# Attention in turns of two head pairs: the order of scores, transposes and weighted sums

## The chip, the cores and the metric

The kernel runs on one core of a Trainium2 chip. The metric is the device time of one execution in microseconds (us), as a median of several runs. Matmuls and transposes run on TensorE (PE), element-wise work on VectorE (DVE), ScalarE (ACT) and GpSimd (POOL); transfers are issued from SyncE (SP) and ACT.

## What is computed

One layer of an encoder block on 1024 tokens of width 1024, a grid of 16 rows by 64 columns:

```python
h = rms_norm(x, norm1_g)
a, gate, q, k, v = split(h @ w_in)
conv_out = conformer_conv(a, gate, ...)             # 31 taps, layer norm, swish
q, k = rms_norm(q per head), rms_norm(k per head)   # 8 heads of 64
attn_out = neighbourhood_attention(q, k, v, rpb)
x = x + concat(conv_out, attn_out) @ w_out
x = x + swiglu(rms_norm(x, norm2_g))                # d_ff 2816
```

In the neighbourhood attention each query attends to 8 rows by 16 columns of keys, clamped inside the grid, with a learned bias by offset, a softmax and a weighted sum of the values:

```python
s = einsum("bqhd,brqchd->bhqrc", q_r, k_win) * scale + bias
p = softmax(s, axis=(-2, -1))
out = einsum("bhqrc,brqchd->bqhd", p, v_win)
```

## The kernel before

Every engine's instructions stay in the order in which the program issues them. A wait at the head of an engine's queue therefore holds all that is behind it on that engine.

The stages follow each other: the input projections with the convolution's taps beside them, the attention, the first output projection, the second norm, the SwiGLU products and the down projection. The stage of this change is the attention, some 80 us of the 1061.5 us of the profile.

There the 1024 queries are cut into 8 blocks of 128 (two halves of the grid's rows by four column blocks). Each block works on 12 grid rows of keys and on a column window of 24 columns for the outer column blocks (288 scores a query) or 32 for the inner ones (384). The blocks with 24 columns come first (`order`, line 600). A block has four head pairs, so there are 32 pairs, numbered `i`; 0 to 15 have 288 scores a row, 16 to 31 have 384.

For one pair:

- `score_mm(i)` (line 603): two matmuls with 64 contraction rows into two PSUM banks of the four that carry the tag `mm` (tile `s`).
- `score_exp(i, ss)` (616): for each head, DVE adds the bias table, writes to the SBUF tile `e` and gives the row's negative maximum (`mx`, line 624). ACT takes the exponential and its sum (626). `e` is a tile of the pool `G`, 128 x 1024 fp32, with 22 buffers.
- `score_norm(i)` (629): DVE's reciprocal of the two sums, POOL's scaling of both halves of `e` (633).
- `flip(i)` (635): six transposes of `e` to the PSUM tile `p`, two banks with the tag `cv`, of which there is a single one.
- `flip_out(i, hh)` (645): the copy of `p` to the SBUF tile `pT`, also of the pool `G`. Half 1 is ACT's, half 0 DVE's. The halves lie interleaved in `pT`:

```python
        (dve.tensor_copy, act.copy)[hh](pTs[i][:, :, hh], pp[i][:m, hh * 512:hh * 512 + 384].rearrange(
            "p (n q) -> p n q", q=P))
```

- `weigh(i)` (650): six matmuls with 64 output columns of `pT` by the values (`vw`), accumulated in the PSUM tile `o` of the block (tag `tp`, two banks).
- After the last pair of a block, `evac_hi` (661, ACT) and `evac_lo` (667, DVE, in two halves) take `o` to SBUF as a rounded part and its rest.

The loop at line 785 does one pair a turn: scores of pair i, transposes and copies of i-2, exponentials of i, weighted sums of i-3. Beside it, `jobs` (a weight split in quarters: a cast on ACT, a subtraction on POOL) go one at a time in two turns of four. After the last scores, `fill` puts the first steps of the output projection between the remaining groups, and then `conv_T` transposes the convolution's output (line 724), the first block of it to the same PSUM tile `cv` that the transposes of the attention use.

Of the kernel before, what the change touches and what calls it, by code (L numbers as in the profile page):

```python
# [12 lines left out]
P = 128  # L13
# [48 lines left out]
def body(tc, a):  # L62
    from contextlib import ExitStack
    with ExitStack() as ctx:
        build(ctx, tc, a)


def build(ctx, tc, a):
    nc = tc.nc
# [6 lines left out]
    def T(tag, shape, bufs, name, dt=F32):  # L76
        return sb.tile(shape, dt, tag=tag, bufs=bufs, name=name)

    def G(name, dt=F32):
        return T("G", [P, 1024], 22, name, dt)  # L80

    def R(name):
        return T("R", [P, 1024], 3, name)
# [7 lines left out]
    def SM(name, n=8):  # L91
        return T("sm", [P, 8], 16, name)[:, :n]

    def mm(name):
        return ps.tile([P, 512], F32, tag="mm", bufs=4, name=name)

    def tp(name):
        return ps.tile([P, 512], F32, tag="tp", bufs=2, name=name)

    def cv(name):  # L100
        return ps.tile([P, 1024], F32, tag="cv", bufs=1, name=name)
# [54 lines left out]
    def take_parts(jobs, n=4, sub=pool):  # L156
        i = pos[1]
        hi, lo = chunks[i][2]()
        w = 1024 // n

        def part(o):
            sl = slice(o, o + w)
            split(hi[:, sl], lo[:, sl], raws[i][:, sl], (sub,))
            if o + w == 1024:
                raws.pop(i)
                issue()
        pos[1] += 1
        jobs.extend(lambda o=o: part(o) for o in range(0, 1024, w))

    def g_pair(name, into):  # L170
        def dst():
            hl = (G(name + "h", F32R), G(name + "l", F32R))
            into.append(hl)
            return hl
        return dst
# [35 lines left out]
    def load_x(t):  # L211
        x_t[t] = G(f"x{t}")
        nc.sync.dma_start(x_t[t], a["x"][t * P:(t + 1) * P, :])

    def load_xt(h, kp, sl):
        if (h, kp) not in xr:
            xr[h, kp] = G(f"xt{h}{kp}").rearrange("p (k s) -> p k s", s=512)
        nc.sync.dma_start(xr[h, kp][:, :, sl], a["xt"][h, kp][:, :, sl])
# [328 lines left out]
    ss = SM("s14", 4)  # L547
# [27 lines left out]
    def table(rh, ty):  # L575
        n = AR * t1[ty].shape[-1]
        src = tf[rh, ty].rearrange("i j h c -> (i j) (h c)")
        if rh == 0 and ty == 0:
            parts = [(G(f"tab{k}")[:, :n * min(3, NH - 3 * k)], 3 * k) for k in range(3)]
        else:  # L580
            parts = [(H(f"tab{rh}{ty}")[:, :NH * n], 0)]
        heads = []
        for w, h0 in parts:
            nc.sync.dma_start(w, src[:, h0 * n:h0 * n + w.shape[-1]])
            heads += [w[:, o:o + n] for o in range(0, w.shape[-1], n)]
        return heads
# [14 lines left out]
    tab, es, pTs, os_, at, sums, pp = {}, {}, {}, {}, {}, {}, {}  # L601

    def score_mm(i):
        s_, hp = divmod(i, 4)
        rh, cb = order[s_]
        t = rh * 4 + cb
        c0, ncol, _ = WIN[cb]
        out = []
        for hh in range(2):
            s = mm(f"s{i}{hh}")[:, :AR * ncol]  # L610
            pe.matmul(s, qT[hh * HD:(hh + 1) * HD, hp, t * P:(t + 1) * P],  # L611
                      k4[hh * HD:(hh + 1) * HD, hp, rh * 4:rh * 4 + AR, c0:c0 + ncol], start=True, stop=True)
            out.append(s)
        return out

    def score_exp(i, ss):
        s_, hp = divmod(i, 4)
        rh, cb = order[s_]
        n = AR * WIN[cb][1]
        e = es[i] = G(f"e{i}").rearrange("p (h n) -> p h n", h=2)[:, :, :n]  # L620
        rs = SM(f"rs{i}", 2)
        for hh in range(2):
            mx = SM(f"mx{i}{hh}", 1)
            dve.tensor_tensor_reduce(out=e[:, hh], in0=ss[hh], in1=tab[rh, cb][2 * hp + hh], scale=-1.0,  # L624
                                     scalar=3.0e38, op0=OP.add, op1=OP.min, accum_out=mx)
            act.activation(e[:, hh], e[:, hh], AF.Exp, bias=mx, scale=-1.0, accum_out=rs[:, hh:hh + 1])  # L626
        sums[i] = rs

    def score_norm(i):
        rs = sums.pop(i)  # L630
        dve.reciprocal(rs, rs)  # L631
        for hh in range(2):
            pool.tensor_scalar(es[i][:, hh], es[i][:, hh], rs[:, hh:hh + 1], 1.0, op0=OP.mult, op1=OP.mult)  # L633

    def flip(i):
        s_, hp = divmod(i, 4)
        m = 4 * WIN[order[s_][1]][1]
        pp[i] = cv(f"p{i}")
        for hh in range(2):
            pt = pp[i][:, hh * 512:hh * 512 + 384]  # L640
            for g in range(3):
                pe.transpose(pt[:m, g * P:(g + 1) * P], es[i][:, hh, g * m:(g + 1) * m], ident)  # L642
        pTs[i] = G(f"pT{i}").rearrange("p (n h q) -> p n h q", h=2, q=P)[:m, :3]

    def flip_out(i, hh):
        m = pTs[i].shape[0]
        (dve.tensor_copy, act.copy)[hh](pTs[i][:, :, hh], pp[i][:m, hh * 512:hh * 512 + 384].rearrange(  # L647
            "p (n q) -> p n q", q=P))

    def weigh(i):  # L650
        s_, hp = divmod(i, 4)
        rh, cb = order[s_]
        if hp == 0:
            os_[s_] = tp(f"o{s_}").rearrange("p (c q) -> p c q", c=4)
        for g in range(3):
            for hh in range(2):
                c = (2 * hp + hh) * HD
                pe.matmul(os_[s_][hh * HD:(hh + 1) * HD, hp], vw[cb, rh + g][:, c:c + HD], pTs[i][:, g, hh],  # L658
                          start=g == 0, stop=g == 2)

    def evac_hi(s_):
        rh, cb = order[s_]
        if rh == 0:
            at[cb] = [G(f"at{cb}{w}", F32R).rearrange("p (c t q) -> p c t q", c=4, t=2) for w in range(2)]
        act.copy(at[cb][0][:, :, rh], os_[s_])

    def evac_lo(s_, cs=slice(0, 4)):
        rh, cb = order[s_]
        hi, lo = [w[:, cs, rh] for w in at[cb]]
        dve.tensor_tensor(lo, os_[s_][:, cs], hi.bitcast(F32), OP.subtract)  # L670
# [5 lines left out]
    jobs = []  # L676

    def load_window(cb):
        for g in range(4):
            load_vw(cb, g)  # L680
# [14 lines left out]
    for g in range(3):  # L695
        load_vw(0, g)
    score_exp(0, s0)
    s1 = score_mm(1)
    value(7)
    score_norm(0)  # L700
    score_exp(1, s1)
    step()
    load_vw(0, 3)
# [12 lines left out]
    def proj(t, d, acc, ks):  # L716
        for k in ks:
            mac(acc, lhs(k, t), wo[d, k], k == 4, k == 3)
            weave()
# [59 lines left out]
    def fill(*ks):  # L779
        if not acc0:  # L780
            act.activation(warm, eps, AF.Sqrt)
            acc0.append(mm("pj0"))
        proj(0, 0, acc0[0], ks)

    for i in range(2, 32 + 2):
        if i == 5:
            tab[0, 1] = tab[0, 2] = table(0, 1)
        if i == 9:
            tab[1, 1] = tab[1, 2] = table(1, 1)
        if i in (6, 12):  # L790
            load_window(i // 6)
        if i in (14, 22):
            take_parts(jobs)
        if i < 32:
            ss = score_mm(i)
        if i >= 32:
            fill(*((4, 5) if i == 32 else (6,)))
        if i < 33:
            score_norm(i - 1)
        flip(i - 2)  # L800
        flip_out(i - 2, 1)
        if i < 32:
            score_exp(i, ss)
        flip_out(i - 2, 0)
        if i > 2:
            weigh(i - 3)
            if i % 4 == 2:
                evac_hi(i // 4 - 1)
            elif i > 6 and i % 4 in (0, 3):
                evac_lo((i + 1) // 4 - 2, slice(0, 2) if i % 4 == 3 else slice(2, 4))  # L810
        if jobs and i % 4 < 2:
            jobs.pop(0)()
    fill(7)

# [401 lines left out]
    for s, p in enumerate(SEQ):  # L1216
        for k in range(QF - 2):
            n = s * QF + k
# [21 lines left out]

# [12 lines left out]
```

## Time and profile before

| | |
|---|---|
| median of 3 runs | 1063.39 us (1062.58 to 1063.52) |
| the profiled execution: time | 1063.23 us |
| its span from the first instruction to the last | 1061.5 us |
| PE busy | 1045.5 us |
| DVE busy | 703.9 us |
| ACT busy | 450.9 us |
| POOL busy | 383.8 us |
| attention, first transposes (pair 0) to the last (pair 31) | 239.65 to 314.01 us |

Times in the rows are us from the span's start unless they are marked ns. A row of the timeline has the start, the duration, the engine, the line, the operation, and output and inputs by the program's names; xN merges N instructions that follow each other. In brackets stands how long the engine was idle before, and what ended that. In the chain of waits each piece starts where the one before ceases to hold the end.

### The profile page before, as it was taken

To read this page: it belongs to the slowest core of one execution; us is meant where nothing else is said; L and a number is where in the kernel's file an instruction comes from. 1 tells how busy PE (TensorE), PEld (TensorE's weight loads), DVE (VectorE), ACT (ScalarE), POOL (GpSimd) and SP (SyncE) were. 2 spreads that over 40 slices of the span, in tenths; PEclk is the share of its full clock that TensorE was granted. 3 is DMA by queue.
4 is the path that set the end of the run, shared out by engine and by line. 5 is a ranking of instruction groups with operands and counts; after the bars stand their busy time and mean duration, and the time that the engine had idled before them with its cause. 6 is when DMAs were issued, how large, how long until landed. Compare 5 with 4: busy or idle time off the path is not lost.

```text
span 1061.5 us, 14053 instructions
## 1 busy us (share of the span) xinstructions
PE 1045.5 (98%) x5068; PEld 847.8 (80%) x5068; DVE 703.9 (66%) x1055; ACT 450.9 (42%) x987; POOL 383.8 (36%) x301
## 2 busy tenths in 40 slices
PE   7999999999999999999999999999999999999997
PEld 6888888876667887788888888888888888888886
DVE  6788987877765257666465564564655567858883
ACT  6456347726766234532323223232233344433441
POOL 0126765523542302444554544545444200002310
PEclk9999999999999999999999999999999999999999
DMA  9416781245504422032322323232231597634541
GB/s 333 165 49 224 223 256 38 77 151 159 165 30 161 137 100 80 23 127 83 134 96 96 109 99 102 97 129 100 70 134 75 198 320 275 208 99 137 188 141 42
DMA packets 68245, 144.06 MB, mean 136 GB/s; under 512 B 12496, under 2 KB 21200, under 8 KB 67536
## 3 DMA queue, kind: packets, MB, share of 16 engines
q1 hardware_dynamic: 66336, 139.95, 39.2%
q10 hardware_dynamic: 1840, 3.22, 0.9%
q8 instruction: 40, 0.66, 0.3%
q14 instruction: 29, 0.24, 0.1%
HBM read 103.99 MB, written 44.76 MB: 140 GB/s over the span
## 4 chain that ended last, share of the span: by engine, by line
PE 92%; DVE 5%; ACT 1%; issue 0%; DMA 0%; SPq 0%; DVEq 0%; ACTq 0%
PE B L113 5%; PE B L114 5%; PE B L112 5%; PE D L112 4%; PE D L114 4%; PE D L113 4%; PE A L112 4%; PE A L113 3%; PE A L114 3%; PE z L112 3%; PE z L113 3%; PE z L114 3%; PE gl L114 3%; PE gl L112 3%; PE gl L113 3%; DVE cv L319 3%
## 5 line engine op out<-in xcount | busy, mean ns | idle before, releaser
L319 DVE SCALAR_TENSOR_TENSOR cv<-u,par,cv 128x1009 f32<-128x1009 f32 (+14 forms) x92 | 117.5, 1277 | 2.4
L345 POOL TENSOR_TENSOR pa<-pa,pr 128x1022 f32<-128x1022 f32 (+5 forms) x24 | 58.0, 2415 | 50.8 <-ACT pr L344 35.2
L104 ACT CAST op<-sr 128x512 fp32r<-128x512 f32 x77 | 47.7, 619 | 50.2 <-PE B2d L114 21.3
L108 DVE TENSOR_TENSOR op<-sr,op 128x512 fp32r<-128x512 f32 x77 | 58.2, 756 | 14.8 <-ACT op L104 14.8
L1036 DVE TENSOR_TENSOR g<-B,g 128x512 f32<-128x512 f32 x22 | 15.2, 690 | 79.0 <-PE B L114 79.0
L1208 POOL TENSOR_TENSOR ou<-ou,resm 128x512 f32<-128x512 f32 x8 | 13.1, 1651 | 142.7 <-ACT op L104 135.0
L1045 ACT ACTIVATE D<-D 128x512 f32<-128x512 f32 x22 | 12.8, 582 | 112.8 <-DVE D L1044 112.8
L1031 DVE TENSOR_TENSOR u<-B,g 128x512 f32<-128x512 f32 x22 | 15.2, 691 | 62.0 <-PE B L114 62.0
L104 ACT CAST op<-wd 128x512 fp32r<-128x512 f32 x66 | 40.9, 619 | 33.5 <-DVE wd L1123 18.6
L108 DVE TENSOR_TENSOR op<-wd,op 128x512 fp32r<-128x512 f32 x66 | 49.7, 753 | 3.0 <-ACT op L104 1.3
L889 DVE TENSOR_TENSOR ts<-gu,ts 128x512 f32<-128x512 f32 x44 | 51.0, 1159 | 0.8
L633 POOL TENSOR_SCALAR e<-e,rs 128x288 f32<-128x288 f32 (+1 forms) x64 | 34.1, 545 | 45.9 <-DVE rs L631 37.1
L1034 ACT ACTIVATE A<-A 128x512 f32<-128x512 f32 x20 | 11.6, 582 | 76.3 <-PE A L114 76.3
L626 ACT ACTIVATE e<-e,mx 128x288 f32<-128x288 f32 (+1 forms) x64 | 36.2, 569 | 7.3 <-DVE mx L624 7.3
L889 DVE TENSOR_TENSOR ts<-gu 128x512 f32<-128x512 f32 x22 | 33.6, 1528 | 0.0
L624 DVE CUSTOM_DVE_ANT_0 e<-s,tab 128x288 f32<-128x288 f32 (+1 forms) x64 | 29.9, 504 | 3.6 <-PE s L611 3.6
L642 PEld LDWEIGHTS p<-ident,e 128*96 128x96 f32 (+1 forms) x192 | 20.1, 133 | 15.0 <-issue 10.4
L372 ACT ACTIVATE sq<-z,r 128x64 f32<-128x64 f32 x96 | 28.6, 334 | 6.5 <-PE z L114 6.5
L642 PE MATMUL p<-ident,e 128*96 128x128 f32 (+1 forms) x192 | 27.6, 280 | 0.6 <-DVE pT L647 0.6
L658 PE MATMUL o<-pT,vw 96*64 96x128 f32 (+1 forms) x384 | 28.0, 281 | 0.0
L611 PE MATMUL s<-kT,qT 64*128 64x288 f32 (+1 forms) x128 | 27.5, 495 | 0.5 <-DVE mx L624 0.5
L344 ACT ACTIVATE pr<-u,par 128x1022 f32<-128x1022 f32 (+5 forms) x24 | 27.0, 1137 | 1.6 <-ACT vs L402 1.6
(1038 smaller groups left out, 3452.6 us busy)
## 6 DMA issues: line engine op xcount, KB each, us to landing
gu<-in_gu SPq DMA_DIRECT2D x44, 512.0 KB
sr<-sd SPq DMA_DIRECT2D x77, 256.0 KB
sd<-sd SPq DMA_DIRECT2D x22, 512.0 KB
wd<-in_wd SPq DMA_DIRECT2D x44, 256.0 KB
sd<-g SPq DMA_DIRECT2D x33, 256.0 KB
x<-in_x SPq DMA_DIRECT2D x16, 512.0 KB
xd<-x SPq DMA_DIRECT2D x8, 512.0 KB
resm<-xd SPq DMA_DIRECT2D x16, 256.0 KB
```

Of the source, the lines that this page charges most:

```text
L104: act.copy(hi, src)
L108: eng.tensor_tensor(*[w[..., sl] for w in (lo, src, hi.bitcast(F32))], OP.subtract)
L112: pe.matmul(acc, lh, rh, start=start, stop=False, skip_group_check=True)
L113: pe.matmul(acc, lh, rl, start=False, stop=False, skip_group_check=True)
L114: pe.matmul(acc, ll, rh, start=False, stop=stop, skip_group_check=True)
L319: dve.scalar_tensor_tensor(acc[:, o], uc[:, i], dwk[:, c, t:t + 1], acc[:, o], OP.mult, OP.add)
L345: pool.tensor_tensor(pa[:, o], pa[:, o], pr[:, o], OP.add)
L624: dve.tensor_tensor_reduce(out=e[:, hh], in0=ss[hh], in1=tab[rh, cb][2 * hp + hh], scale=-1.0, scalar=3.0e38, op0=OP.add, op1=OP.min, accu ...
L626: act.activation(e[:, hh], e[:, hh], AF.Exp, bias=mx, scale=-1.0, accum_out=rs[:, hh:hh + 1])
L633: pool.tensor_scalar(es[i][:, hh], es[i][:, hh], rs[:, hh:hh + 1], 1.0, op0=OP.mult, op1=OP.mult)
L642: pe.transpose(pt[:m, g * P:(g + 1) * P], es[i][:, hh, g * m:(g + 1) * m], ident)
L889: dve.tensor_tensor(o, l, r, OP.subtract)
```

## The change

The loop takes two pairs a turn (i = 2, 4, ... 32): scores of i and i+1, transposes of i-2, weighted sums of i-3 and i-2, transposes of i-1. `score_exp` can be called for one head, and its calls are placed between the copies: first head 0 of pair i, then ACT's copy of pair i-2, then head 1 of pair i and head 0 of pair i+1, then DVE's copy of pair i-2; head 1 of pair i+1 and the normalization of pair i come after the weighted sums. The evacuations of `o` and the weight split come at the end of a turn. The bias tables are asked for at i = 4 and 8 (before: 5 and 9). The pool `G` has 24 buffers (before: 22), for which the reserve of SBUF for the DMA descriptors that software makes is set to 64 bytes a partition.

```diff
     def G(name, dt=F32):
-        return T("G", [P, 1024], 22, name, dt)
+        return T("G", [P, 1024], 24, name, dt)
...
-    def score_exp(i, ss):
+    def score_exp(i, ss, heads=(0, 1)):
...
-        e = es[i] = G(f"e{i}").rearrange("p (h n) -> p h n", h=2)[:, :, :n]
-        rs = SM(f"rs{i}", 2)
-        for hh in range(2):
+        if i not in es:
+            es[i] = G(f"e{i}").rearrange("p (h n) -> p h n", h=2)[:, :, :n]
+            sums[i] = SM(f"rs{i}", 2)
+        e, rs = es[i], sums[i]
+        for hh in heads:
...
-    for i in range(2, 32 + 2):
-        if i == 5:
+    for i in range(2, 32 + 2, 2):
+        last = i == 32
+        if i == 4:
             tab[0, 1] = tab[0, 2] = table(0, 1)
-        if i == 9:
+        if i == 8:
             tab[1, 1] = tab[1, 2] = table(1, 1)
...
-        if i < 32:
-            ss = score_mm(i)
-        if i >= 32:
-            fill(*((4, 5) if i == 32 else (6,)))
-        if i < 33:
-            score_norm(i - 1)
+        ss = [] if last else [score_mm(i), score_mm(i + 1)]
+        if last:
+            fill(4, 5)
+        score_norm(i - 1)
         flip(i - 2)
+        if not last:
+            score_exp(i, ss[0], (0,))
         flip_out(i - 2, 1)
-        if i < 32:
-            score_exp(i, ss)
+        if not last:
+            score_exp(i, ss[0], (1,))
+            score_exp(i + 1, ss[1], (0,))
         flip_out(i - 2, 0)
         if i > 2:
             weigh(i - 3)
-            if i % 4 == 2:
-                evac_hi(i // 4 - 1)
-            elif i > 6 and i % 4 in (0, 3):
-                evac_lo((i + 1) // 4 - 2, slice(0, 2) if i % 4 == 3 else slice(2, 4))
-        if jobs and i % 4 < 2:
+        if last:
+            fill(6)
+        weigh(i - 2)
+        if not last:
+            score_exp(i + 1, ss[1], (1,))
+            score_norm(i)
+        flip(i - 1)
+        flip_out(i - 1, 1)
+        flip_out(i - 1, 0)
+        if i % 4 == 2 and i > 2:
+            evac_hi(i // 4 - 1)
+        if i > 4:
+            evac_lo((i + 2) // 4 - 2, slice(0, 2) if i % 4 == 2 else slice(2, 4))
+        if jobs:
             jobs.pop(0)()
     fill(7)
...
-    nc = bacc.Bacc("TRN2", target_bir_lowering=False, num_devices=1)
+    nc = bacc.Bacc("TRN2", target_bir_lowering=False, num_devices=1, dynamic_dma_scratch_size=64)
```

More of the change, by code (lines that the diff above doesn't have):

```diff
@@ L626, in score_exp @@
             act.activation(e[:, hh], e[:, hh], AF.Exp, bias=mx, scale=-1.0, accum_out=rs[:, hh:hh + 1])
-        sums[i] = rs
     def score_norm(i):
```

## The prediction

> **What bounds the kernel now.** I read the page first: the engines' shares and the granted clock.
>
> ```profile
> span 1061.5 us, 14053 instructions
> ...
> PE 1045.5 (98%) x5068; PEld 847.8 (80%) x5068; DVE 703.9 (66%) x1055; ACT 450.9 (42%) x987; POOL 383.8 (36%) x301
> ...
> PEclk9999999999999999999999999999999999999999
> ```
>
> TensorE (PE) is busy for 98% of the span at full granted clock, so whatever is added between two of its instructions is added to the end. The second view is the table of windows; a stretch of the attention stage shows (busy us of PE, weight load, DVE, ACT, POOL, then clock):
>
> ```profile
> 290.00:300.00 10.00, 10.00 (x96) 6.47 (x92) 7.61 (x28) 7.95 (x25) 6.10 (x11) 1.00 0.15 50
> ```
>
> PE has no gap there, while DVE and ACT are at 76% and 80%. These two are close enough to full that their order inside a turn matters. The third view, the chain of waits in order of time, shows how long each group of PE work lasts. I call a pair's two score matmuls S (line 611), its six transposes F (642), its weighted sums W (658), ACT's and DVE's copies of the transposes A and D (647). D writes the half `hh` 0, A the half 1 of the same tile.
>
> ```profile
> 238.97 0.69 PE s L611 x4
> 239.65 0.81 PE p L642 x6
> 240.54 0.48 ACT pT L647
> 241.04 0.56 DVE pT L647
> 241.74 0.83 PE p L642 x6
> ...
> 257.08 0.69 PE s L611 x4
> 257.77 0.79 PE p L642 x6
> 258.56 0.81 PE o L658 x12
> ...
> 285.49 0.85 PE s L611 x4
> 286.34 0.81 PE p L642 x6
> 287.15 0.81 PE o L658 x12
> ...
> 308.46 0.81 PE p L642 x6
> ...
> 314.01 0.66 PE p L642 x6
> ...
> 316.38 0.44 PE y L724 x4
> ```
>
> Columns: start, duration, who. A pair costs 0.69 + 0.79 + 0.81 = 2.29 us with the narrow windows (288 scores a row, pairs 0 to 15) and 0.85 + 0.81 + 0.81 = 2.47 with the wide ones (384). All of it is PE's own work. The first five rows are the one place where PE must wait for the copies: F(0) starts at 239.65, A(0) follows 0.89 later, D(0) 0.50 after A(0), and F(1), which needs the same PSUM tile, 0.70 after D(0). From the start of F to the first PE instruction that needs both copies are 0.89 + 0.50 + 0.70 = 2.09 us. D does not run beside A, it runs behind it. The list of waits says so too (waiter, awaited: us, times, longest):
>
> ```profile
> DVE pT L647 <- ACT pT L647: 7.0, 16, 1.7
> ```
>
> After its start-up the old order hides the 2.09: behind F(i) come W(i-1), S(i+3), F(i+1), W(i), so W(i) starts 0.79 + 0.81 + 0.69 + 0.79 = 3.08 us after F(i), and F(i+1) 0.79 + 0.81 + 0.69 = 2.29 after it.
>
> **The change, part by part.** A turn (even i) becomes, on PE: S(i), S(i+1), F(i-2), W(i-3), W(i-2), F(i-1). I use line numbers of before.
>
> *Fewer group changes.* Transposes that follow their like or long matmuls without an edge take 0.66 for six (row 314.01), between S and W 0.79: an edge of some 0.13. If merging two W saves one edge and nothing else, PE's turn is 2 x 0.69 + 0.79 + 0.81 + 0.66 + 0.79 = 4.43 narrow, against 2 x 2.29 = 4.58, and 2 x 0.85 + 0.81 + 0.81 + 0.66 + 0.81 = 4.79 wide against 4.94. Over 14 turns (6 narrow, 8 wide) that is 14 x 0.15 = 2.1 us; the edges F to S and W to F that the new order has are not in the trace, nearest are these, and if two whole edges go each turn it is 14 x 0.26 = 3.6. The Trainium skill, TensorEngine Tiling (Array Packing), Key Properties, says that a change of tiling mode drains TensorE; scores (64 rows), transposes and sums (64 columns) are three modes, so by that rule alone the change is faster. The rows agree that there is an edge.
>
> *W(i-2) now follows F(i-2) with only W(i-3) between.* That is a cover of 0.79 + 0.81 = 1.60 against the 2.09 that the two copies need: PE idles at least 0.49 a turn, even if ACT and DVE are free when F ends. This already exceeds the edge saved. Behind the waiting W stand F(i-1) and everything else of PE.
>
> *ACT and DVE are not free then.* Both engines keep their program order. On ACT the new order is E(i,0), A(i-2), E(i,1), E(i+1,0), E(i+1,1), A(i-1), then evac_hi's cast and a weight cast; E is the exponential (626). On DVE: reciprocal(i-1), T(i,0), T(i,1), T(i+1,0), D(i-2), T(i+1,1), reciprocal(i), D(i-1), L; T is the bias and maximum (624), L the half evacuation of line 670. So A(i-2) stands behind E(i,0), that behind T(i,0), that behind reciprocal, L and D(i-1) of the turn before, and D(i-1) behind A(i-1) and F(i-1). F(i-1) in turn stands behind W of its turn. This closes a loop, F(i-1) to F(i+1), that runs once a turn. Its links, start to start:
>
> ```profile
> 254.59 0.55 DVE L647 COPY pT<-p 96x384 f32<-96x384 f32 x1 [0.30 <-ACT pT L647]
> 255.07 0.41 DVE L670 TENSOR_TENSOR at<-o,at 128x256 fp32r<-128x256 f32 x1
> 255.64 0.17 DVE L631 RECIPROCAL rs<-rs 128x2 f32<-128x2 f32 x1 [0.16 <-ACT e L626]
> 255.79 0.46 DVE L624 CUSTOM_DVE_ANT_0 e<-s,tab 128x288 f32<-128x288 f32 x1
> ```
>
> ```profile
> 232.04 0.45 DVE L624 CUSTOM_DVE_ANT_0 e<-s,tab 128x288 f32<-128x288 f32 x1
> ...
> 232.59 0.54 ACT L626 ACTIVATE e<-e,mx 128x288 f32<-128x288 f32 x1 [6.82 <-DVE mx L624]
> ```
>
> ```profile
> 259.56 0.52 ACT L626 ACTIVATE e<-e,mx 128x288 f32<-128x288 f32 x1
> 259.98 0.19 ACT L626 ACTIVATION_READ_ACCUMULATOR e<-e,mx 128x1 f32 x1
> 260.07 0.57 ACT L665 CAST at<-o 128x512 fp32r<-128x512 f32 x1
> ```
>
> ```profile
> L624 DVE CUSTOM_DVE_ANT_0 e<-s,tab x64: 439/505/558, 232.0 to 309.2; 128x288 f32<-128x288 f32 x32, 128x384 f32<-128x384 f32 x32
> L626 ACT ACTIVATE e<-e,mx x64: 520/568/619, 232.6 to 310.3; 128x288 f32<-128x288 f32 x32, 128x384 f32<-128x384 f32 x32
> ```
>
> F to A 0.89; A to D 0.50; D to L 0.48 (254.59 to 255.07); L to reciprocal 0.33 (its 0.41 less the 0.07 by which the next instruction overlapped D; an estimate); reciprocal to T 0.15; T to E 0.55 (232.04 to 232.59); E to the next on ACT 0.51 (259.56 to 260.07); A(i-2) to D(i-2) 0.50; D(i-2) to W(i-2) 0.70; W to F 0.83 (a group begun after a wait took 0.83 in row 241.74; W alone 0.66 to 0.84). Sum 5.44 us. With wide windows T and E are each longer, by the least and largest of the last two rows 0.10 and, as the next group starts before its end, some 0.09: 5.63. Both exceed PE's 4.43 and 4.79, so the loop sets the pace and PE idles 1.01 and 0.84 us a turn before W(i-2). S(i), S(i+1), F(i-2), W(i-3), 1.38 + 0.79 + 0.81, lie in its shadow.
>
> The sum from F(1) to F(29) (rows 241.74 and 308.46): 14 loops, 6 narrow, of which the first two have no L (0.33 less), 8 wide: 2 x 5.11 + 4 x 5.44 + 8 x 5.63 = 77.0 us. Before 66.7. Added: 10.3. Both spans hold 28 W.
>
> *The first turn* has no W(i-3): S(2) at 238.97, F(0) 1.38 later at 240.35, W(0) 2.09 later at 242.44, F(1) 0.83 later at 243.27, against 241.74: added 1.5.
>
> *The end.* After F(29) one W less is left (0.81 gained). The first four transposes of line 724 need the PSUM tile that D(31) empties. They started 2.37 after F(31) (314.01 to 316.38), with W(30) between, which now lies ahead of F(31): 1.56 by PE, 2.09 by the copies, so 0.5 is lost. Net 0.3 gained.
>
> *What costs nothing.* The scaling on POOL for F(i) now starts in the turn before, a whole S, S earlier than its use. Tables and value windows are asked for at most a pair earlier; no wait of PE in this stage ends on a DMA. The weight casts go from two pairs in four to one a turn, after A(i-1), where ACT has some 1.6 us until E(i+2,0). The four score banks are all taken each turn; S(i+2) follows T(i+1,1) by more than a group. The two more wide tiles hold one more e and one more pT, which the new order keeps alive. The reserve for software DMA descriptors shrinks, and the page's queues are hardware and instruction queues alone. Later stages are PE's own work, so the shift is carried to the end undiminished.
>
> Total: 10.3 + 1.5 - 0.3 = 11.5, from a span of 1061.5 to 1073.0. The profiled execution took 1063.23, 1.7 more than its span and 0.2 less than the median 1063.39. Forecast: 1074.9 us, 1.1% slower.
>
> **The rivals.** *Only the bare latency (chance 0.06).* If ACT came free in time, the turn would be 1.38 + 2.09 + 0.83 + 0.79 = 5.09 narrow and 1.70 + 2.10 + 0.83 + 0.81 = 5.44 wide: 74.1 against 66.7, with the ends 8.6 more, 1072.0. Against it: E(i,0) stands ahead of A(i-2) in program order.
>
> *No stall, edges saved (0.06): not slower.* If the copies were hidden, 2.1 to 3.6 us go: 1059.8 to 1061.3, faster by 0.2 to 0.3%. It decides where A and D together take under 1.60 us from F's start. Only running them side by side could do that, and the row 7.0, 16 speaks against it. This is also where the Trainium skill's drain rule would end if nothing else counted.
>
> *A buffer wait (0.03).* If the new e tile of pair i took the buffer that F(i-2) still reads, T(i,0) would wait for F(i-2): turn 1.38 + (0.89 + 0.55 + 0.51 + 0.50 + 0.70) + 0.83 + 0.79 = 6.15, wide 6.68, 25 us more, 1088. Against it: the number of tiles grows by just what the order needs.
>
> *The clock falls (0.02).* If PE's pauses of 1 us lowered its clock to half in the stage, its 4.43 and 4.79 would double and pass the loop: 6 x 8.86 + 8 x 9.58 = 129.8, some 63 more, 1126. Against it: no slice of the clock row is under 9. The Trainium skill, TensorE: Matmul & The Clock Gate, A second HAM failure mode, tells of short pauses between groups that throttled a kernel; no row here shows it.
>
> **How the numbers follow.** The loop has 0.83. Its own range: terms read from single rows, 0.3 a turn either way (L 0.33 or 0.41, W 0.66 or 0.84, a few hundredths for each wait), is 4 us: 1071 to 1079. The bare latency lies inside; a little more room above for waits not seen gives 1071 to 1080. Within 0.2% (2.1 us), about what can be told from no change, lies at most the near end of the second rival: same 0.01, faster 0.05, slower 0.94.
>
> **What would show it.** After the change the windows of the attention stage should show PE busy some 80 to 85% and DVE and ACT a lower share than before; the list of waits should name W (line 659 then) waiting for pT's copies on DVE some 15 times, about 1 us each, where none did; F(i-1) to F(i) should take about 2.2 us and F(i) to F(i+1) 3.3 (2.5 and 3.1 wide), together 5.4 then 5.6; A(i-2) should start right after E(i,0). The forecast is wrong if D starts before A's end, if the two F distances add to under 5.0, or if the time is gained back in another stage.

## The result and the profile after

The changed kernel takes 1073.64 us (median of 5, 1073.53 to 1073.91) against 1063.39 (1062.58 to 1064.02) of the kernel before on the same chip: 1.0098 times as long, 95% interval 1.0087 to 1.0108. The profiled execution took 1073.65 us with a span of 1071.7, against 1063.23 and 1061.5.

First the page of the kernel after: span, busy time with share and instructions of each engine, PE's busy share in 40 slices, and the granted clock.

```profile
span 1071.7 us, 14103 instructions
...
PE 1043.5 (97%) x5068; PEld 848.3 (79%) x5068; DVE 702.8 (66%) x1055; ACT 451.6 (42%) x987; POOL 383.7 (36%) x301
...
PE   7999999998889999999999999999999999999997
...
PEclk9999999999999999999999999999999999999999
```

PE has the same 5068 matmuls and is busy 2.0 us less than before, while the span is 10.2 us longer: the time went into pauses. They lie in slices 10 to 12, the only ones inside the span under 9; at 26.8 us a slice these cover 241 to 322 us, the attention stage. The clock row doesn't fall.

The same stretch of the attention stage in the table of windows (busy us of PE, weight load, DVE, ACT, POOL, then clock, DMA share, GB/s), and the list of waits (waiter, awaited: us in all, times, longest):

```profile
290.00:300.00 10.00, 9.11 (x84) 6.25 (x86) 6.29 (x25) 6.77 (x21) 5.42 (x9) 1.00 0.25 85
```

```profile
DVE pT L648 <- ACT pT L648: 35.7, 32, 2.5
...
PE o L659 <- DVE pT L648: 10.6, 15, 1.2
```

The window had 10.00 us of PE work (x96) before and has 9.11 (x84). DVE fell from 76% to 63%, ACT from 80% to 68%: they, too, do less in the same time. DVE now waits for ACT's copy for every one of the 32 pairs, 35.7 us where it was 7.0 for 16, and the weighted sums (659) wait for DVE's copy 15 times, 0.7 us each on average; before there was no such line.

One turn in the chain of waits, from F(i-1) to F(i+1):

```profile
258.70 0.79 PE p L643 x6
259.49 0.73 PE s L611 x4
...
261.45 0.63 ACT e L628 x2
262.08 0.37 ACT pT L648
...
262.47 0.56 DVE pT L648
...
263.08 0.88 PE o L659 x12
263.95 0.80 PE p L643 x6
```

And what DVE and ACT did in between, from the timeline of the same kernel:

```profile
260.03 0.55 DVE L648 COPY pT<-p 96x384 f32<-96x384 f32 x1 [1.81 <-ACT pT L648]
260.51 0.41 DVE L671 TENSOR_TENSOR at<-o,at 128x256 fp32r<-128x256 f32 x1
260.84 0.15 DVE L632 RECIPROCAL rs<-rs 128x2 f32<-128x2 f32 x1
260.91 0.43 DVE L626 CUSTOM_DVE_ANT_0 e<-s,tab 128x288 f32<-128x288 f32 x1
```

```profile
259.53 0.47 ACT L648 COPY pT<-p 96x384 f32<-96x384 f32 x1 [0.72 <-PE p L643]
261.45 0.54 ACT L628 ACTIVATE e<-e,mx 128x288 f32<-128x288 f32 x1 [1.45 <-DVE mx L626]
261.89 0.19 ACT L628 ACTIVATION_READ_ACCUMULATOR e<-e,mx 128x1 f32 x1
261.98 0.46 ACT L648 COPY pT<-p 96x384 f32<-96x384 f32 x1
```

Read them as one path: F(i-1) at 258.70, A(i-1) 259.53, D(i-1) 260.03, L 260.51, reciprocal 260.84, T(i,0) 260.91, E(i,0) 261.45, A(i-2) 261.98, D(i-2) 262.47, W(i-2) 263.08, F(i+1) 263.95. ACT is idle for 1.45 us ahead of E(i,0), though F(i-2) is about to hand it a copy; the copy stands behind that exponential in ACT's order. PE resumes 0.61 us after D(i-2) starts.

Where the 10.2 us of span went is read off the chain at the two ends of the stage:

```profile
239.23 1.53 PE s L611 x8
240.75 0.81 PE p L643 x6
...
243.63 0.80 PE p L643 x6
```

```profile
318.63 0.81 PE p L643 x6
...
326.06 0.66 PE y L725 x4
```

F(1) starts 1.89 later than before (243.63, 241.74). From F(1) to F(29) it is 75.00 us, before 66.72: 8.28 more. From F(29) to the first transposes of the convolution 7.43, before 7.92: 0.49 less. Together 9.68 (316.38 to 326.06). The last 0.5 of the span comes behind that: the seventh group of the convolution's transposes (725) starts 10.24 later than before (338.62, 328.38). The first and the fourth of these groups give 0.22 each, with 0.66 us where they took 0.44. After them nothing is added and nothing is gained back.

### The profile page after: what moved, and what is told of

It is laid out like the page before. It is cut to its first block, busy times and chain, and to the rows that moved or that the text cites. A ratio compares the mean times of both kernels' runs of the same rounds, so it can differ in the third digit from the quotient of the medians.

```text
span 1071.7 us, 14103 instructions
## 1 busy us (share of the span) xinstructions
PE 1043.5 (97%) x5068; PEld 848.3 (79%) x5068; DVE 702.8 (66%) x1055; ACT 451.6 (42%) x987; POOL 383.7 (36%) x301
## 4 chain that ended last, share of the span: by engine, by line
PE 85%; DVE 7%; ACT 3%; issue 2%; DMA 1%; POOL 0%; SPq 0%; DVEq 0%; ACTq 0%; POOLq 0%
PE B L113 5%; PE B L114 5%; PE B L112 5%; PE D L112 4%; PE D L114 4%; PE D L113 4%; PE A L112 3%; PE A L114 3%; PE A L113 3%; PE gl L114 3%; PE gl L113 3%; PE gl L112 3%; DVE cv L319 3%; PE z L112 2%; PE z L114 2%
## 5 line engine op out<-in xcount | busy, mean ns | idle before, releaser
L648 DVE COPY pT<-p 96x384 f32<-96x384 f32 (+1 forms) x32 | 17.8, 555 | 35.7 <-ACT pT L648 35.7
L659 PEld LDWEIGHTS o<-pT,vw 96*64 96x64 f32 (+1 forms) x384 | 20.3, 136 | 17.6 <-DVE pT L648 14.6
```

## The experiments

The experiments are called e1 to e9 in the text. Line numbers of the kernels with split tiles (e2, e3, e6, e9) are one more than those above, those of e7 one more than in the kernel before.

**The copy before the exponential (e1).** ACT is given A(i-2) ahead of E(i,0), and nothing else is changed. That opens the loop.

```diff
-        if not last:
-            score_exp(i, ss[0], (0,))
         flip_out(i - 2, 1)
         if not last:
+            score_exp(i, ss[0], (0,))
             score_exp(i, ss[0], (1,))
```

> The changed kernel with one edit: on ACT the copy A(i-2) is issued ahead of the exponential E(i,0). Theory 1 (the loop over DVE's and ACT's queues sets the turn): the links T(i,0) to E(i,0) to A(i-2) leave the loop, what is left is F(i-1), S, F(i-2), A(i-2), D(i-2), W(i-2): with the links of the changed kernel's trace 0.79 + 1.31 + 0.83 + 0.50 + 0.61 + 0.88 = 4.92 us a narrow turn (it was 5.26) and some 5.28 a wide one (5.53): 3.5 us less in the stage, 1070.2 us. Theory 2 (the two copies' own latency behind F already set the stall, the queues do not matter): no change, 1073.6. Theory 3 (PE itself is dearer in the new order: edges between groups, or scores that wait for their four banks): no change, 1073.6.

Measured: 1069.55 us, 1.0056 of before (1.0043 to 1.0070). F(odd) to F(odd) is 4.89 to 4.95 us narrow and 5.18 to 5.22 wide, where the changed kernel has 5.25 to 5.30 (4.90 without L) and 5.46 to 5.57. In a narrow turn its chain has neither T nor E nor L:

```profile
258.92 1.17 PE s L611 x8
...
260.16 0.85 PE p L643 x6
...
261.08 0.48 ACT pT L648
...
261.59 0.56 DVE pT L648
...
262.19 0.88 PE o L659 x12
263.07 0.79 PE p L643 x6
```

What is left there is the bare latency: F(i-2) at 260.16, A, then D, and W(i-2) 2.03 later, with only W(i-3) to cover it. In the last narrow turn and in the wide ones what ends last is again a queue, now DVE's alone: D(i-1), then L, the reciprocal and three T stand ahead of D(i-2).

```profile
284.76 0.55 DVE pT L648
...
285.74 0.45 DVE e L626
286.20 0.47 DVE e L626
286.68 0.47 DVE e L626
287.16 0.48 DVE pT L648
287.69 0.88 PE o L659 x12
```

The bare latency lies close behind it: ACT's copy of that pair runs from 286.54 to 287.02, so it ends some 0.1 us before D begins.

So to have A(i-2) behind E(i,0) cost 4.1 of the 10.2 us. That T and E leave the path gives no more than this, some 0.33 us a turn, because these two paths lie only that much below the loop; the first two turns, whose loop has no L, take 4.89 to 4.90 us with and without the edit.

**The two copies side by side (e2).** D stood behind A although they read different banks, because both banks were one PSUM tile. Now each half has its own tile; to keep the number of banks, the scores of odd pairs take the two-bank tile.

```diff
+        cc = cv(f"s{i}") if i % 2 and i > 1 else None
         for hh in range(2):
-            s = mm(f"s{i}{hh}")[:, :AR * ncol]
+            s = (cc[:, hh * 512:] if cc is not None else mm(f"s{i}{hh}"))[:, :AR * ncol]
...
-        pp[i] = cv(f"p{i}")
+        pp[i] = [mm(f"p{i}{hh}") for hh in range(2)]
```

> The changed kernel with the two halves of the transposes in two PSUM tiles of one bank each (from the four score banks) in place of one tile of two banks; the scores of the odd pair take the two-bank tile instead. D(i-2) then no longer stands behind A(i-2). ACT's order is as in the changed kernel. Theory 1 (loop): the loop without the link A to D is 0.83 + 0.48 + 0.33 + 0.07 + 0.54 + 0.53 + 0.59 + 0.88 = 4.25 us narrow, under PE's own 4.4, so PE is without gaps again; 14 turns cost 6 x 4.45 + 8 x 4.76 = 64.8 us against 75.0 in the changed kernel and 66.7 before; with the start and the end 1062 us, within 0.2% of before. Theory 2 (bare latency of the copies): only the 0.50 us of one copy a turn goes, 1066. Theory 3 (PE's edges or the score banks): no change, 1073.6.

Measured: 1062.62 us, 0.9994 (0.9985 to 1.0003): no difference from before, and 11.0 us less than the changed kernel. The timeline shows ACT's copy running inside DVE's:

```profile
258.91 0.47 ACT L649 COPY pT<-p 96x384 f32<-96x384 f32 x1
```

```profile
258.76 0.55 DVE L649 COPY pT<-p 96x384 f32<-96x384 f32 x1
```

In the list of waits DVE's copies no longer wait for ACT. The Trainium skill, PSUM — Partial Sum Buffer, Specifications (TRN2), says that ScalarE and VectorE can access PSUM in parallel at full bandwidth as long as there is no bank collision. This pair of rows agrees for two banks: 0.47 and 0.55 us side by side, where the copies one behind the other took 0.48 and 0.55 or 0.56. The wait before was thus one of the tile, not of the banks.

The time was as expected, but not the way to it. Expected were turns without a stall; measured were turns of 4.21 us in alternation with 4.83 (wide 4.60 and 5.21, once 5.73, at i = 20). The long ones are those in which a block ends, and their chain shows why:

```profile
252.12 0.47 ACT pT L649
252.59 0.49 ACT at L667
...
253.11 0.07 DVE at L672
...
254.72 0.47 DVE pT L649
...
255.24 0.88 PE o L660 x12
256.12 0.79 PE p L644 x6
256.91 1.17 PE s L612 x8
258.08 0.79 PE p L644 x6
258.87 1.46 PE o L660 x24
260.33 0.80 PE p L644 x6
```

The half evacuation L (672) waits for ACT's cast evac_hi (667), which stands behind A(i-1); the reciprocal, three T and D(i-2) stand behind L. The last five rows are a turn without that: PE's own work, 4.21 us with no gap.

**Both edits together (e3).** On top of the split tiles:

```diff
         flip(i - 2)
-        if not last:
-            score_exp(i, ss[0], (0,))
         flip_out(i - 2, 1)
         if not last:
+            score_exp(i, ss[0], (0,))
             score_exp(i, ss[0], (1,))
```

> Both edits: two PSUM tiles for the halves of the transposes, and A(i-2) ahead of E(i,0) on ACT. Theory 1 (loop): PE is the bound already with the split alone, so this adds nothing: within 0.5 us of the split, 1062. If E(i,0) ahead of A(i-2) still costs PE something after the split, this is faster than the split by that. Theory 2: 1066 or less. Theory 3: 1073.6.

Measured: 1064.91 us, 1.0013 (1.0004 to 1.0022). The expectation failed: the edit that saved 4.1 us before costs 2.3 here. Turns are 4.21 and 5.03, wide 4.60 and 5.39 to 5.67. The chain of a long turn:

```profile
260.02 2.18 ACT e L629 x8
262.20 0.36 ACT pT L649
262.57 0.49 ACT at L667
```

ACT now waits at its head for the transposes (22.0 us over 22 copies of the stage, 5.8 over 16 without the edit) while the exponentials that it could do stand behind. Four of them, 2.18 us, then come in a row ahead of A(i-1), the cast and L, which the next turn waits for. With the loop gone, the first order was the better one.

**The old order with the tiles, and with the split (e5, e7).** Two controls: the kernel before with the two more wide tiles and the smaller reserve (e5), and the kernel before with the halves split (e7).

> The kernel before with only the two more wide tiles (24) and the smaller reserve for software DMA descriptors, in the old order of one pair a turn. All theories of the order: no change, within 0.1% of 1063.4. If instead the reserve or the placement of tiles in SBUF costs the time, it shows here: up to 1073.

> The old order of one pair a turn with the same two PSUM tiles for the halves of the transposes (scores of odd pairs in the two-bank tile). Theory 1: in the old order the copies lie in the shadow of PE, so the split buys nothing there but the 0.5 us of the first turn: 1063 us, turns of 4.56 and 4.91 us for two pairs as before. Otherwise (the split is worth something by itself, not through the wait of W on the copies): as much faster as the split made the new order beyond it.

Measured: 1063.23 us, 0.9998 (0.9989 to 1.0007), and 1063.03, 0.9995 (0.9986 to 1.0004). Neither matters to the old order; the 10.2 us belong to the new one. The split does what it should there too (ACT's copies wait for PE alone, and DVE's for ACT never), but the old order had the 2.09 us covered already.

**The evacuation moved (e8, e6).** The first half of L goes from the end of the turn in which the block ends to the next turn, behind that turn's `score_norm(i)`; the second half stays at the next turn's end. First on the changed kernel (e8), then on the split one (e6).

```diff
             score_norm(i)
+        if i > 4 and i % 4 == 0:
+            evac_lo(i // 4 - 2, slice(0, 2))
         flip(i - 1)
...
-        if i > 4:
-            evac_lo((i + 2) // 4 - 2, slice(0, 2) if i % 4 == 2 else slice(2, 4))
+        if i > 4 and i % 4 == 0:
+            evac_lo(i // 4 - 2, slice(2, 4))
```

> The changed kernel, transposes in one PSUM tile as it has them, with only evac_lo moved as in the last-but-one kernel. Theory 1 (loop over D(i-1), L, reciprocal, T, E, A(i-2), D(i-2), W(i-2)): the six loops that begin in a turn where a block ends lose the link L, 0.34 us each: the turns alternate between 5.27 and 4.93 narrow, 5.51 and 5.17 wide, 2.0 us in all: 1071.6. Theory 2 (PE's order or the bare latency sets the turn): no change, 1073.6.

Measured: 1071.38 us, 1.0073 (1.0059 to 1.0086). Turns go 4.93 to 4.95 without L in the loop and 5.25 with it (wide 5.16 to 5.20 and 5.45 to 5.52): L's price in the loop is 0.3 us a turn, as the prediction had it.

> The split kernel (two PSUM tiles for the halves of the transposes) with one more edit: the first half of evac_lo (L, a subtraction on DVE) leaves the end of the turn in which a block ends, where it waits for evac_hi's cast on ACT with the next turn's T's behind it, and goes to the next turn behind the second scaling. Theory 1 (what is left of the loop in the split kernel is this wait, in every second turn): all turns take PE's own time, 4.21 us narrow and 4.60 wide, in place of 4.83 and 5.21 in every second: F(1) to F(29) 6 x 4.21 + 8 x 4.60 = 62.1 us against 66.3 in the split kernel, 1058.4 us, 0.5% faster than before. Theory 2 (the longer turns come from ACT being full in these turns, with the cast and four exponentials): the turns stay at 4.83 and 5.21, 1062.6.

Measured: 1062.08 us, 0.9988 (0.9979 to 0.9997), with single runs from 1060.74 to 1063.97, short of the 1058.4 that were expected. The alternation is gone, so it came from the wait of L, as theory 1 had it, and not from a full ACT: all turns but one are 4.21 to 4.31 and 4.60 to 4.70. But the turn at i = 20 takes 7.06. What is late there is a transfer. First its piece in the chain, then SP's issues and DVE's T(20,0) in the timeline:

```profile
264.21 17.11 DMA tab<-tf
```

```profile
246.75 17.36 SPq L596 DMA_DIRECT2D vw<-vd  x4
264.21 2.40 SPq L584 DMA_DIRECT2D tab<-tf  x1
```

```profile
281.49 0.56 DVE L627 CUSTOM_DVE_ANT_0 e<-s,tab 128x384 f32<-128x384 f32 x1 [2.92 <-DMA tab<-tf]
```

T(20) is the first that uses the bias table of the inner column blocks in the second half of rows. That table is asked for at 264.21, behind 17.36 us in which SP issues a window of values, because `load_window(1)` is called at i = 6 and the table at i = 8; it lands at 281.32. With the shorter turns T(20) is ready before that and waits. In e2 the table was asked for at 264.79, and T(20,0) starts at 282.00 after 0.42 us of idle time; the same wait would explain its one turn of 5.73, but that profile does not name it.

**The table before the window (e9).** To the last kernel one more line:

```diff
-        if i in (6, 12):
-            load_window(i // 6)
+        if i in (8, 12):
+            load_window(i // 4 - 1)
```

> The split kernel with evac_lo moved, and one more edit: the value windows of the third column block are asked for at i = 8, behind the bias table of the last blocks, in place of i = 6, ahead of it. In the split kernel with evac_lo moved, one turn (i = 20) took 7.06 us: DVE's T(20,0) waited for that table, whose transfer was issued at 264.2 behind the windows on SP's queue and landed 17.1 later. Theory 1 (that queue order is the last stall): the turn takes 4.60 like its neighbours, 2.4 us less: 1059.6 us, 0.35% faster than before. Theory 2 (the table is late for another reason, its own 17 us or a buffer it waits for): the stall stays or moves to the windows, 1062.

Measured: 1059.52 us (1059.03 to 1060.00), 0.9965 of before (0.9952 to 0.9977), faster than both kernels. A stretch of the stage in the table of windows:

```profile
290.00:300.00 10.00, 10.00 (x98) 6.99 (x98) 7.96 (x31) 8.63 (x26) 6.66 (x12) 1.00 0.10 36
```

PE is full again, with x98 matmuls recorded in 10 us where it was x96 before: most turns are 4.21 and 4.60 us where two old ones were 4.54 to 4.57 and 4.89 to 4.92. F(1) to F(29) takes 63.00 us (before 66.72, changed 75.00). One turn, at i = 12, still has 0.7 us of stall, and it too ends on a table:

```profile
262.14 0.46 DVE L627 CUSTOM_DVE_ANT_0 e<-s,tab 128x288 f32<-128x288 f32 x1 [1.17 <-DMA tab<-tf]
```

The transfer that this T waits for was issued at 246.07, after SP had spent 17.20 us on the windows ahead of it.

## Why the prediction was right, and where its numbers were off

**The mechanism held.** The forecast was 1074.9 us, measured were 1073.64. The sum came this near in part because its errors offset each other: the loop was set 2.1 us too high and the end's gain 0.2 too low, while 0.4 at the start and 0.5 behind the stage were missing. W(i-2) waits for D 15 times; A(i-2) starts right behind E(i,0) (261.98 after 261.45); D never starts before A ends; the clock stays at 1.00. F(i-1) to F(i) takes 2.1 us and F(i) to F(i+1) 3.2 (wide 2.3 and 3.2), where the forecast had 2.2 and 3.3 (2.5 and 3.1). That the loop is what sets the pace, and not merely a path that fits, is shown by e1, which opens it and gains 4.1 us, and by e8, which takes L out of every other turn and gains 0.3 in just these.

**The loop's links were too long by some 0.2 us a turn.** Predicted and measured, in the order of the prediction: F to A 0.89, 0.83; A to D 0.50, 0.50; D to L 0.48, 0.48; L to reciprocal 0.33, 0.33; reciprocal to T 0.15, 0.07; T to E 0.55, 0.54; E to A 0.51, 0.53; A to D 0.50, 0.49; D to W 0.70, 0.61; W to F 0.83, 0.87. Sum 5.44, 5.25 (4.90 in the two turns without L). The largest miss, D to W, was taken from a row in which transposes, not weighted sums, waited for D. Two turns without L were 0.21 shorter than predicted, four narrow ones 0.17, eight wide ones 0.12 (means): 2.1 of the 77.0 us, so the loop added 8.3 and not 10.3.

**The start was worth 1.9, not 1.5.** Of this 0.26 lies ahead of the stage (S(2) at 239.23 instead of 238.97). The scores of pairs 2 and 3 took 1.53 us where 2 x 0.69 was set.

**The end gave 0.5 instead of 0.3**, and the later stages carried the shift undiminished, as assumed; the 0.5 more arise in the convolution's transposes right behind it.

**The share of PE in the stage** was forecast at 80 to 85%; the window shows 91%, another of ten us at 260 shows 84%. The pauses counted (0.7 us of 5.25 on average) say 87%; the forecast had 1.01 of 5.44.

**Off the path, one term was mis-sized:** what merging saves. The prediction took 0.15 to 0.26 a turn, one or two edges of 0.13. Without stalls PE's turn is 4.21 and 4.60, 0.35 and 0.31 less than two old ones: S of two pairs takes 1.17 where two took 1.38, W of two pairs 1.46 (wide 1.50) where two took 1.62. It made no difference while the loop set the pace: the order that saves 0.35 us of PE a turn made PE wait 0.7 us for the copies.

**The rivals.** Bare latency is what ends last in most of e1's narrow turns, 4.89 to 4.95 us against the 5.09 worked out, and lies some 0.1 us behind what does in its wide ones, 5.2 against 5.44; in the changed kernel the loop lies some 0.33 above it. No stall needed the copies side by side, as the rival said; with them so, and two later waits taken away, e9 has its gain, 3.7 us where 2.1 to 3.6 were set. No turn comes near the 6.15 us of a buffer wait, and the old order with the same tiles is unchanged. The clock never fell.

**What stays open:** why two groups of the convolution's transposes are 0.22 us longer each after the change, and what sets the 15.9 and 17.1 us from a table's issue to its landing in e9 and e6.

## What to carry to other kernels

When a reorder brings a consumer close behind its producer, write down each helper engine's queue and look for a chain that leads from one turn's work round to the next turn's: the turn can't be shorter than it, however little each engine is busy. The two readers of one PSUM tile waited for each other here although their banks differ, so a tile shared between two engines is worth splitting as soon as its latency shows. And a wait removed uncovers the next: here the copies, then the cast ahead of the evacuation, then a table queued behind a window; an order that helps while one wait rules (e1) can cost time once it is gone (e3).

## What was not expected of the hardware

Groups of small matmuls got cheaper per pair by merging more than the 0.13 us edge read from the transposes: 0.21 us for eight score matmuls in a row, 0.16 (wide 0.12) for 24 weighted sums. And a pause of PE in every turn of some 5.3 us, 15 in all of 0.34 to 1.21 us and twelve of them of 0.64 to 0.79, left the granted clock at 1.00 all through the stage. The Trainium skill, TensorE: Matmul & The Clock Gate, A second HAM failure mode, describes pauses between groups that throttled another kernel, which no row here shows.
